# Attention in a two-layer hybrid backbone: queries split once and placed by transfers, the result norm taken for two heads at a time, its epsilon term summed by TensorE

## The chip, the cores and the metric

The kernel runs on one core of a Trainium2 chip. The metric is the time of one execution in device microseconds, as the median of several runs. The engines of the core work side by side, each on its own list of instructions in a fixed order, and wait for each other through semaphores: TensorE (PE in the profile; PEld is its weight load), VectorE (DVE), ScalarE (ACT), GpSimd (POOL) and SyncE (SP), whose list here holds only the starts of transfers.

## The reference, cut to what matters

Two layers of a backbone over 512 latent and 256 context tokens. Between one input projection and one output projection stand three groups of heads; the change touches group B, differential attention with 4 heads of two softmax maps each. In layer 0 the context tokens attend among themselves as well; in the last layer they only give keys and values.

```python
def diff_attn(q, k, v, lam):
    s = jnp.einsum("bqhmd,bkhmd->bhmqk", q.astype(F32), k.astype(F32)) * (B_QK_DIM ** -0.5)
    p = jax.nn.softmax(s, axis=-1)
    a = p[:, :, 0] - lam * p[:, :, 1]
    return jnp.einsum("bhqk,bkhd->bqhd", a, v.astype(F32))

def rms_norm(x, g):
    xf = x.astype(F32)
    y = xf * lax.rsqrt(jnp.mean(xf * xf, axis=-1, keepdims=True) + EPS)
    return (y * g.astype(F32)).astype(x.dtype)

def mixer_merge(pa, o, pc, P, lam_init):
    ...
    yb = (rms_norm(o, P["subln_g"]) * (1.0 - lam_init)).astype(pa.dtype).reshape(b, n, B_WIDTH)
    ...
    return jnp.concatenate([ya, yb, yc], axis=-1) @ P["w_out"]
```

`o` is what attention returns, and `rms_norm(o, subln_g)` is the result norm that the title speaks of.

## The kernel before, in words

A scheduler gives each engine the order of its instructions when the kernel is built, from priorities and a cost model of its own; the order is then fixed. Matrix products with weights or activations in fp32r use a split of each operand into a high part and the rest (`mm3`, L225 to L228: three products), so that every weight tile is loaded as `raw`, cast to `whi` by ACT and has its rest `wlo` taken by DVE or POOL (`wsplit`).

**The attention stage** (L712 to L870) stands once in each layer between the last input projection and the output projection. Its unit of work is a pair (head h, block p of 256 queries), and each pair has two units of 128 queries. Layer 0 has 12 pairs: first the 4 heads of the context block (`p == 2`, 256 keys), then 8 latent pairs (768 keys). Layer 1 has only the 8 latent pairs. The text calls them context pairs and latent pairs.

For each pair:

- `q_prep`: two transposes (L737) put the pair's queries into `pq` in PSUM, with the 64 rows of map 0 above the 64 rows of map 1. `qh` holds the high part of one map twice, in the upper and the lower 64 partitions, and `qlz` holds the rest of one map in the half in which that map's rows stand; the other half of `qlz` is zero (written once, L720 and L724). For this ACT copies `pq` to `qn` (L747), two of the four placing copies run on ACT and two on POOL (L751), and DVE takes two rests (L754, which the trace shows on L106). For the first pair all four copies are ACT's (L741).
- `scores`: for each of the two maps, `pss` = kk·qh (L768) + kk·qlz (L769), the row maximum on DVE (`mx`, L771), the exponential with its sum on ACT (`e`; the trace shows all activations of the helper on L97). `pss` has two buffers.
- `combine`: e0 + cc·e1 on DVE (L787), where `cc` comes from the two sums; POOL fills `dg` (L788), a diagonal with the epsilon of the norm times the squared sum.
- `transp`: transposes of `e` (`pat`, L109), 6 for a latent unit, copied to `ath`: the first four by ACT (L804), the last two by DVE (L806).
- `attn_v`: `po` = vt·ath (L816), copied to `o` and squared to `osq` by ACT (L819, L820), and POOL adds `dg` to it (L821).
- `subln`: `pr` = ones·osq (L828) sums over the 128 features; ACT takes logarithm and exponential, DVE scales (`o`, L831), ACT casts `yBh` (L833), DVE takes the rest `yBl` (L834, on L106 in the trace).

Between these TensorE gets filler: `wout(mp2, (0,), ...)`, the part of the output projection that needs only the other head groups (`yACh`, `yACl`), 12 products of one width for each tile `wo`. Layer 0 has 2 of the 4 column groups as filler, layer 1 has 3. DVE adds each finished `wo` tile to `xT` (L704). After the stage the output projection goes on with its remaining parts.

SP's list holds every transfer in one order. During the stage these are the loads of `w_out` tiles (`raw`, 3 buffers), and behind them, for layer 0, loads of modulation weights (`mraw`).

## Time and profile before

| what | us |
|---|---|
| median of 3 runs | 1638.32 (1637.74 to 1638.40) |
| profiled execution | 1637.72, its span 1635.9 |
| attention stage, layer 0 | 246.5 to 354.7 of the span |
| attention stage, layer 1 | 1143.25 to about 1230 of the span |

The profile is of one execution. A busy share counts the time in which an engine has an instruction under way. TensorE's matmuls overlap, so a duration in its rows is longer than the step from one start to the next; what a matmul costs in a chain is read from the starts. The granted clock is a share of TensorE's full speed.

### The profile page before, as it was taken

The page shows a single profiled execution, that of the slowest core. Times are in us where ns is not written, and L with a number is a line of the kernel's source. Part 1 is how long each engine was busy: PE and PEld are TensorE (multiplying, and loading weights), DVE is VectorE, ACT ScalarE, POOL GpSimd, SP SyncE. Part 2 cuts the span into 40 slices and gives each one's busy share as a digit, 9 for nine tenths or more (in the row PEclk, how much of TensorE's full clock was granted, in tenths as well). Part 3 has the DMA queues.
Part 4 walks back from the last instruction along what each step waited for, and adds up shares of the span by engine and source line. Part 5 has one row for each costly group of instructions (what it writes and reads, how often), then busy time and mean ns, then how long its engine had stood idle before and what let it go on. Part 6 is the DMA issues. An engine that isn't in the chain of part 4 may idle for free.

```text
span 1635.9 us, 20796 instructions
## 1 busy us (share of the span) xinstructions
PE 1574.7 (96%) x8186; PEld 1294.7 (79%) x8186; DVE 1033.9 (63%) x1666; ACT 646.2 (40%) x1098; POOL 178.3 (11%) x158
## 2 busy tenths in 40 slices
PE   7999998999999999999999999779999999999999
PEld 5865776778888888888888878567778788888888
DVE  4597878969999862244333277996987544244433
ACT  5431568753523221133232244255775433123321
POOL 1130224310000000000000023341420000000000
PEclk8999999999999999999999999889999999999999
DMA  8625110014355852111122223221001223332232
GB/s 286 201 96 171 42 62 14 14 64 169 104 193 194 290 192 70 66 65 62 56 65 58 84 87 110 62 65 52 27 27 65 91 90 96 88 101 97 96 100 94
DMA packets 57409, 162.08 MB, mean 99 GB/s; under 512 B 9056, under 2 KB 11360, under 8 KB 57184
## 3 DMA queue, kind: packets, MB, share of 16 engines
q1 hardware_dynamic: 57312, 160.76, 30.3%
q8 instruction: 64, 1.05, 0.3%
q14 instruction: 33, 0.27, 0.0%
HBM read 158.64 MB, written 2.10 MB: 98 GB/s over the span
## 4 chain that ended last, share of the span: by engine, by line
PE 83%; DVE 10%; ACT 4%; issue 1%; DMA 1%; POOL 0%; POOLq 0%; DVEq 0%; SPq 0%; ACTq 0%
PE pp L227 13%; PE pp L226 13%; PE pp L228 13%; PE pd L228 6%; PE pd L226 6%; PE pd L227 6%; PE acc L389 4%; PE acc L390 4%; PE acc L397 3%; DVE cacc L647 3%; PE po L816 2%; PE mr L156 2%; PE wo L226 1%; PE wo L227 1%; PE wo L228 1%
## 5 line engine op out<-in xcount | busy, mean ns | idle before, releaser
L220 ACT CAST whi<-raw 128x1024 fp32r<-128x1024 f32 (+2 forms) x199 | 204.3, 1029 | 550.9 <-PE pp L227 251.0
L106 DVE TENSOR_TENSOR wlo<-raw,whi 128x1024 fp32r<-128x1024 f32 (+1 forms) x163 | 196.9, 1210 | 304.9 <-ACT whi L220 297.4
L227 PE MATMUL pp<-hlo,whi 128*128 128x512 f32 (+1 forms) x1072 | 380.7, 356 | 0.8 <-DVE hlo L266 0.8
L226 PE MATMUL pp<-hhi,whi 128*128 128x512 f32 (+1 forms) x1072 | 379.8, 356 | 1.5 <-ACT whi L220 1.3
L228 PE MATMUL pp<-hhi,wlo 128*128 128x512 f32 (+1 forms) x1072 | 378.9, 354 | 0.0
L226 PEld LDWEIGHTS pp<-hhi,whi 128*128 128x128 f32 x1072 | 201.4, 188 | 35.1 <-ACT whi L220 2.7
L227 PEld LDWEIGHTS pp<-hlo,whi 128*128 128x128 f32 x1072 | 201.5, 188 | 33.0 <-DVE hlo L266 1.5
L228 PEld LDWEIGHTS pp<-hhi,wlo 128*128 128x128 f32 x1072 | 201.5, 188 | 31.0
L106 POOL TENSOR_TENSOR wlo<-raw,whi 128x1024 fp32r<-128x1024 f32 (+1 forms) x36 | 100.3, 2788 | 870.3 <-ACT whi L220 716.9
L228 PE MATMUL pd<-gh,wlo 128*128 128x512 f32 (+1 forms) x550 | 192.4, 350 | 0.6 <-DVE wlo L106 0.6
L226 PE MATMUL pd<-gh,whi 128*128 128x512 f32 (+1 forms) x550 | 192.9, 351 | 0.0
L227 PE MATMUL pd<-gl,whi 128*128 128x512 f32 (+1 forms) x550 | 192.3, 350 | 0.0
L389 PE MATMUL acc<-whi,hhi 128*128 128x512 f32 x352 | 144.8, 411 | 2.8 <-ACT whi L220 2.8
L390 PE MATMUL acc<-whi,hlo 128*128 128x512 f32 x352 | 144.2, 410 | 0.0
L647 DVE SCALAR_TENSOR_TENSOR cacc<-cin,cw,cacc 128x783 f32<-128x783 f32 (+1 forms) x120 | 125.8, 1102 | 2.8 <-ACT cacc L642 2.7
L228 PEld LDWEIGHTS pd<-gh,wlo 128*128 128x128 f32 x550 | 103.4, 188 | 15.9 <-DVE wlo L106 0.8
L227 PEld LDWEIGHTS pd<-gl,whi 128*128 128x128 f32 x550 | 103.5, 188 | 15.1
L226 PEld LDWEIGHTS pd<-gh,whi 128*128 128x128 f32 x550 | 103.4, 188 | 14.9
L983 DVE TENSOR_TENSOR ft<-ft,pp 128x256 f32<-128x256 f32 (+1 forms) x66 | 39.4, 598 | 96.2 <-PE pp L228 84.7
L397 PE MATMUL acc<-wlo,hhi 128*128 128x512 f32 x352 | 94.0, 401 | 0.0
L389 PEld LDWEIGHTS acc<-whi,hhi 128*128 128x128 f32 x352 | 68.0, 193 | 25.0 <-issue 7.1
L192 DVE CUSTOM_DVE_ANT_0 mraw<-mraw,csil,bmod 128x1024 f32<-128x1024 f32 x64 | 81.7, 1280 | 8.0 <-DMA mraw<-in_w_modT_dram 7.8
(198 smaller groups left out, 2334.3 us busy)
## 6 DMA issues: line engine op xcount, KB each, us to landing
raw<-in_w_gv_dram SPq DMA_DIRECT2D x88, 512.0 KB, 3.2
mraw<-in_w_modT_dram SPq DMA_DIRECT2D x64, 512.0 KB, 4.2
raw<-in_w_in_dram SPq DMA_DIRECT2D x44, 512.0 KB, 3.6
raw<-in_w_down_dram SPq DMA_DIRECT2D x34, 512.0 KB, 3.6
mraw<-in_w_modN_dram SPq DMA_DIRECT2D x16, 512.0 KB, 5.9
mraw<-in_w_modH_dram SPq DMA_DIRECT2D x16, 512.0 KB, 3.9
raw<-in_w_out_dram SPq DMA_DIRECT2D x16, 512.0 KB, 3.2
raw<-in_w_down_dram SPq DMA_DIRECT2D x16, 384.0 KB, 3.2
```

What stands on the lines that cost most here:

```text
L106: (eng or V).tensor_sub(o, a, hi.bitcast(F32))
L156: T.matmul(o[r:r + 32], cs[:, k], w, start=k < 4, stop=k >= 4, tile_position=(0, r))
L192: r = V.tensor_tensor_reduce(out=junk, in0=w, in1=csil[:, s], scale=1.0, scalar=bmod[:, l, i, f:f + 1], op0=ALU.mult, op1=ALU.add, accum_o ...
L220: S.copy(hi, raw)
L226: T.matmul(o, lhi, rhi, start=start, stop=False)
L227: T.matmul(o, lhi, rlo, start=False, stop=False)
L228: T.matmul(o, llo, rhi, start=False, stop=stop)
L389: T.matmul(pt[t], hhi[hs], wh[:, a], start=k2 + a == 0, stop=False)
L390: T.matmul(pt[t], hlo[hs], wh[:, a], start=False, stop=False)
L397: T.matmul(pt[t], hhi[hs], wl[:, a], start=False, stop=k2 + 1 == KD // 2 and a == 1)
L647: V.scalar_tensor_tensor(out=cacc[:, c, :cn], in0=cin[:, c, j:j + cn], scalar=cw[:, l, c, j:j + 1], in1=cacc[:, c, :cn], op0=ALU.mult, op1 ...
L983: V.tensor_mul(t[:, a:b], t[:, a:b], pp[s][1][:, :b - a])
```

## The change

The zeroed buffers go. `q_prep` casts the pair's queries once to `qn[:, 0]` (ACT) and takes the rest once to `qn[:, 1]` (DVE); four transfers on the sync queue then place both parts of each map in both halves of `qq`. The rest thus stands in both halves too. `qq` has three buffers and `qn` two. `dg` has 5 buffers instead of 3. In `transp` the second copy (L806 before) goes to ACT for the second unit of each pair. In `attn_v` only the copy to `o` is left, into one half of a tile for two pairs. `subln` runs once for two pairs (two heads of the same block): one square, one logarithm, one exponential, one scaling, one cast and one rest, each 512 wide instead of 256; POOL's addition of `dg` to `osq` goes, and TensorE adds ones·dg into `pr` by a second matmul for each pair.

```diff
-            qlz = [sp.tile([P, 2, 256], F32R, name=f"qlz{x}") for x in range(2)]
-            zero = sp.tile([P, 256], F32, name="zero")
-            G.memset(zero, 0.0)
-            for x in qlz:
-                for m in range(2):
-                    ms = slice((1 - m) * QKD, (2 - m) * QKD)
-                    G.tensor_copy(x[ms, m], zero[ms])
...
             def q_prep(n):
                 h, p = pairs[n]
-                qh = sp.tile([P, 2, 256], F32R, tag="qh", name="qh", bufs=QB)
-                ql = qlz[n % 2]
+                qq = sp.tile([P, 2, 2, 256], F32R, tag="qq", name="qq", bufs=QB)
+                qn = sp.tile([P, 2, 256], F32R, tag="qn", name="qn", bufs=2)
                 pq = ps.tile([P, 256], F32, tag="w", name="pq", bufs=WB)
                 for i in range(2):
                     T.transpose(pq[:, i * P:(i + 1) * P], qt[2 * p + i][:, h * P:(h + 1) * P], ident)
-                if n == 0:
-                    for m in range(2):
-                        for a in range(2):
-                            S.copy(qh[a * QKD:(a + 1) * QKD, m], pq[m * QKD:(m + 1) * QKD])
-                    for m in range(2):
-                        ms = slice(m * QKD, (m + 1) * QKD)
-                        sub_lo(ql[ms, m], pq[ms], qh[ms, m])
-                else:
-                    qn = sp.tile([P, 256], F32R, tag="qn", name="qn", bufs=2)
-                    S.copy(qn, pq)
-                    for m in range(2):
-                        src = qn[m * QKD:(m + 1) * QKD]
-                        for a in range(2):
-                            (G.tensor_copy if a else S.copy)(qh[a * QKD:(a + 1) * QKD, m], src)
-                    for m in range(2):
-                        ms = slice(m * QKD, (m + 1) * QKD)
-                        sub_lo(ql[ms, m], pq[ms], qn[ms])
-                st["q", n] = (qh, ql)
+                S.copy(qn[:, 0], pq)
+                sub_lo(qn[:, 1], pq, qn[:, 0])
+                for m in range(2):
+                    for a in range(2):
+                        nc.sync.dma_start(out=qq[a * QKD:(a + 1) * QKD, :, m].bitcast(F32), in_=qn[m * QKD:(m + 1) * QKD].bitcast(F32))
+                st["q", n] = (qq[:, 0], qq[:, 1])
...
-                    if c0 == 0:
+                    if c0 == 0 or i == 1:
                         S.copy(at[osl], pat[:, :cn_])
                     else:
                         V.tensor_copy(at[osl], pat[:, :cn_])
...
-                o = sp.tile([P, 256], F32, tag="o", name="o", bufs=2)
-                sq = sp.tile([P, 256], F32, tag="osq", name="osq", bufs=2)
-                S.copy(o, po)
+                if n % 2 == 0:
+                    st["sub", n // 2] = sp.tile([P, 2, 256], F32, tag="o", name="o", bufs=2)
+                S.copy(st["sub", n // 2][:, n % 2], po)
+
+            def subln(x):
+                h, p = pairs[2 * x]
+                o = st["sub", x]
+                sq = sp.tile([P, 2, 256], F32, tag="osq", name="osq", bufs=2)
                 S.activation(sq, o, AF.Square)
-                G.tensor_add(sq, sq, st["dg", n].rearrange("p a q -> p (a q)"))
-                st["sub", n] = (o, sq)
-
-            def subln(n):
-                h, p = pairs[n]
-                o, sq = st["sub", n]
-                pr = ps.tile([P, 256], F32, tag="w", name="pr", bufs=WB)
-                T.matmul(pr, ones, sq, start=True, stop=True)
+                pr = ps.tile([P, 2, 256], F32, tag="w", name="pr", bufs=WB)
+                for y in range(2):
+                    T.matmul(pr[:, y], ones, sq[:, y], start=True, stop=False)
+                    T.matmul(pr[:, y], ones, st["dg", 2 * x + y].rearrange("p a q -> p (a q)"), start=False, stop=True)
                 act(sq, pr, AF.Ln, scale=1.0 / P)
                 act(sq, sq, AF.Exp, scale=-0.5)
                 V.scalar_tensor_tensor(out=o, in0=o, scalar=gsub, in1=sq, op0=ALU.mult, op1=ALU.mult)
-                ts = slice(p * 256, p * 256 + 256)
-                S.copy(yBh[:, h, ts], o)
-                sub_lo(yBl[:, h, ts], o, yBh[:, h, ts])
+                osl = (slice(None), slice(h, h + 2), slice(p * 256, p * 256 + 256))
+                S.copy(yBh[osl], o)
+                sub_lo(yBl[osl], o, yBh[osl])
...
-                if 0 <= v < nu and units[v][1] == 1:
-                    subln(units[v][0])
+                if 0 <= v < nu and units[v][1] == 1 and units[v][0] % 2 == 1:
+                    subln(units[v][0] // 2)
```

The order of the other work moves with it, at three places above all. **The start of the stage in layer 0, on TensorE.** A row is line, operation, output and inputs; `pq` are query transposes, `wo` filler, `pss` scores. Before, from the last two transposes on:

```order
L737 MATMUL pq<-ident,q_1271 128x128
L737 MATMUL pq<-ident,q_1272 128x128
L226 MATMUL wo<-yACh,whi 128x256
L227 MATMUL wo<-yACl,whi 128x256
L228 MATMUL wo<-yACh,wlo 128x256
L768 MATMUL pss<-kk,qh 128x256
L226 MATMUL wo<-yACh,whi 128x256
```

Now, at the same place, the end of the filler that stands between the transposes and the first scores:

```order
L228 MATMUL wo<-yACh,wlo 128x512
L226 MATMUL wo<-yACh,whi 128x512
L227 MATMUL wo<-yACl,whi 128x512
L750 MATMUL pss<-kk,qq 128x256
L751 MATMUL pss<-kk,qq 128x256
L228 MATMUL wo<-yACh,wlo 128x512
```

Three filler products stood between the last transpose and the first score; now 20 do, 12 of width 256 and 8 of width 512. In all, 66 filler products of layer 0 (36 of width 256, 30 of width 512) stand ahead of the first latent score now, 18 of width 512 in the latent pairs, and none behind the last score. In layer 1, 16 of width 512 stand ahead of the first score, where 2 did, and 12 behind the last, where 25 did.

**The end of the stage in layer 0, on TensorE.** Here `pat` are transposes of `e`, `po` the products with the values, `pr` the sums of the norm. Before:

```order
L109 MATMUL pat<-ident,e 128x128 x6
L227 MATMUL wo<-yACl,whi 128x512
L228 MATMUL wo<-yACh,wlo 128x512
L816 MATMUL po<-ath,vt 128x256 x6
L828 MATMUL pr<-osq,ones 128x256
L226 MATMUL wo<-yACh,whi 128x512
L227 MATMUL wo<-yACl,whi 128x512
L228 MATMUL wo<-yACh,wlo 128x512
L226 MATMUL wo<-yACh,whi 128x512
L828 MATMUL pr<-osq,ones 128x256
```

Now:

```order
L109 MATMUL pat<-ident,e 128x128 x6
L798 MATMUL po<-ath,vt 128x256 x6
L811 MATMUL pr<-osq,ones 128x256
L812 MATMUL pr<-dg,ones 128x256
L811 MATMUL pr<-osq,ones 128x256
L812 MATMUL pr<-dg,ones 128x256
L226 MATMUL wo<-yACh,whi 128x256
L227 MATMUL wo<-yACl,whi 128x256
```

The filler between and behind the last sums is gone from here, and each pair's sum is followed by the product with `dg`.

**SP's queue in layer 0**, from the last loads of the input projection on. Before:

```order
L212 DMA raw<-in_w_in_dram 128x2x512 x4
L212 DMA raw<-in_w_out_dram 128x1024 x7
L189 DMA mraw<-in_w_modT_dram 128x1024 x2
L212 DMA raw<-in_w_out_dram 128x1024
L189 DMA mraw<-in_w_modT_dram 128x1024
```

Now:

```order
L212 DMA raw<-in_w_in_dram 128x2x512 x4
L212 DMA raw<-in_w_out_dram 128x1024 x5
L736 DMA qq<-qn 64x2x256 x12
L212 DMA raw<-in_w_out_dram 128x1024
L736 DMA qq<-qn 64x2x256 x20
L212 DMA raw<-in_w_out_dram 128x1024
L736 DMA qq<-qn 64x2x256 x16
L189 DMA mraw<-in_w_modT_dram 128x1024 x2
```

The 48 placing transfers of layer 0 stand in one queue with the last two weight loads between them, each of which waits for a `raw` buffer, and ahead of the modulation loads.

## Rows read from the trace of the kernel before

**Rows 1.** The profile page: part 1 (busy time, share of the span and instructions of each engine), and the shares by engine in the chain that ended last.
```profile
PE 1574.7 (96%) x8186; PEld 1294.7 (79%) x8186; DVE 1033.9 (63%) x1666; ACT 646.2 (40%) x1098; POOL 178.3 (11%) x158
...
PE 83%; DVE 10%; ACT 4%; issue 1%; DMA 1%; POOL 0%; POOLq 0%; DVEq 0%; SPq 0%; ACTq 0%
```

**Rows 2.** Busy time by stretch: start and end of the stretch, its length, busy time and instructions of each engine, granted clock, share of the transfer engines, GB/s. First the context pairs, the latent pairs and the tail of layer 0, then start, latent pairs and tail of layer 1.
```profile
246.50:266.90 20.40, 16.32 (x86) 13.04 (x85) 16.36 (x49) 16.78 (x58) 10.87 (x23) 0.83 0.08 27
266.90:339.50 72.60, 67.02 (x370) 55.41 (x370) 67.14 (x128) 57.65 (x140) 24.91 (x38) 1.00 0.03 8
339.50:354.70 15.20, 13.72 (x65) 10.33 (x63) 8.93 (x18) 9.69 (x22) 2.31 (x4) 1.00 0.00 1
...
1143.25:1147.50 4.25, 3.49 (x17) 2.16 (x16) 2.04 (x6) 3.93 (x11) 3.77 (x5) 1.00 0.11 29
1147.50:1219.00 71.50, 67.45 (x364) 55.32 (x363) 66.95 (x123) 54.09 (x124) 25.77 (x39) 1.00 0.06 21
1219.00:1232.80 13.80, 12.90 (x59) 10.25 (x58) 7.58 (x13) 9.19 (x18) 1.45 (x2) 1.00 0.12 39
```

**Rows 3.** The groups of VectorE and ScalarE that the change touches, and one row of a wider kind, in the stage of layer 0 (244 to 354), shapes kept apart: busy time, mean ns of one, then idle time before them.
```profile
L106 DVE TENSOR_TENSOR qlz<-pq,qn 64x256 fp32r<-64x256 f32 x22 | 9.2, 418 | 0.4
L831 DVE SCALAR_TENSOR_TENSOR o<-o,gsub,osq 128x256 f32<-128x256 f32 x12 | 7.1, 594 | 2.9 <-ACT osq L97 2.8
L806 DVE COPY ath<-pat 128x256 f32<-128x256 f32 x16 | 6.5, 413 | 1.7 <-PE pat L109 1.6
L106 DVE TENSOR_TENSOR yBl<-o,yBh 128x256 fp32r<-128x256 f32 x11 | 4.6, 419 | 1.7 <-ACT yBh L833 1.6
L704 DVE SCALAR_TENSOR_TENSOR xT<-wo,modv,xT 128x512 f32<-128x512 f32 x4 | 3.0, 745 | 0.4 <-PE wo L228 0.3
L804 ACT COPY ath<-pat 128x256 f32<-128x256 f32 x8 | 3.0, 371 | 1.3 <-PE pat L109 1.2
L751 ACT CAST qh<-qn 64x256 fp32r<-64x256 f32 x22 | 8.9, 404 | 0.3
L747 ACT CAST qn<-pq 128x256 fp32r<-128x256 f32 x11 | 4.0, 378 | 0.6 <-PE pq L737 0.5
```

**Rows 4.** A subtraction of width 512 on VectorE, from its timeline: start, duration, engine, line.
```profile
374.30 0.69 DVE L249 TENSOR_TENSOR nss<-nss,nsq 128x512 f32<-128x512 f32 x1
```

**Rows 5.** POOL's addition to the squares in the same stretch of layer 0, in the form of rows 3, and from the list of waits TensorE's for POOL's placing copies (us in total, times, longest).
```profile
L821 POOL TENSOR_TENSOR osq<-osq,dg 128x256 f32<-128x256 f32 x12 | 10.6, 885 | 23.8 <-ACT osq L820 23.8
...
PE pss L768 <- POOL qh L751: 1.6, 2, 1.1
```

**Rows 6.** TensorE's timeline in the tail of layer 0: start, duration, line, operation, and in brackets what ended an idle time ahead of it. `x12`, `x2` count the instructions of a row; an fp32 product of the program is two of them.
```profile
342.17 2.86 PE L816 MATMUL po<-ath,vt 128*128 128x256 f32 x12
344.86 0.59 PE L828 MATMUL pr<-osq,ones 128*128 128x256 f32 x2
345.30 0.82 PE L109 MATMUL pat<-ident,e 128*128 128x128 f32 x6
345.87 0.48 PE L227 MATMUL wo<-yACl,whi 128*128 128x512 f32 x1
...
351.32 0.70 PE L828 MATMUL pr<-osq,ones 128*128 128x256 f32 x2 [0.41 <-POOL osq L821]
...
352.31 0.40 PE L226 MATMUL wo<-yACh,whi 128*128 128x512 f32 x1
352.55 0.40 PE L227 MATMUL wo<-yACl,whi 128*128 128x512 f32 x1
...
354.71 0.39 PE L226 MATMUL wo<-yACh,whi 128*128 128x256 f32 x1 [0.84 <-DVE xT L704]
```

**Rows 7.** TensorE's timeline over one latent pair of layer 0, from one pair's first score after a sum to the next: its two ends, its filler and its idle time.
```profile
298.66 0.58 PE L768 MATMUL pss<-kk,qh 128*128 128x512 f32 x1
...
301.06 0.48 PE L228 MATMUL wo<-yACh,wlo 128*128 128x512 f32 x1
...
301.83 0.48 PE L226 MATMUL wo<-yACh,whi 128*128 128x512 f32 x1
...
302.38 0.40 PE L228 MATMUL wo<-yACh,wlo 128*128 128x512 f32 x1
303.77 0.47 PE L768 MATMUL pss<-kk,qh 128*128 128x512 f32 x1 [0.99 <-ACT e L97]
...
308.50 0.58 PE L768 MATMUL pss<-kk,qh 128*128 128x512 f32 x1
```

**Rows 8.** TensorE's timeline ahead of the stage in layer 0, two filler products of width 256, and the first complete scores of layer 1.
```profile
245.08 0.28 PE L226 MATMUL wo<-yACh,whi 128*128 128x256 f32 x1
245.20 0.28 PE L227 MATMUL wo<-yACl,whi 128*128 128x256 f32 x1
...
1143.25 0.82 PE L737 MATMUL pq<-ident,q 128*128 128x128 f32 x6
...
1146.69 0.51 PE L769 MATMUL pss<-kk,qlz 128*128 128x512 f32 x1 [0.72 <-POOL qlz L724]
```

**Rows 9.** Transfers: tensors, queue, count, KB each, median us from issue to landing; and from SP's timeline two issues in a row (start, duration).
```profile
out_dram<-xT SPq DMA_DIRECT2D x4, 128.0 KB, 1.8
lq<-in_lam_qk_dram SPq DMA_DIRECT2D x2, 128.0 KB, 3.7
...
357.13 0.90 SPq L189 DMA_DIRECT2D mraw<-in_w_modT_dram  x2
```

More of the change, by code (lines that the diff above doesn't have):

```diff
@@ L781, in combine @@
                 if i == 0:
-                    st["dg", n] = sp.tile([P, 2, P], F32, tag="dg", name="dg", bufs=3)
+                    st["dg", n] = sp.tile([P, 2, P], F32, tag="dg", name="dg", bufs=5)
                 dg = st["dg", n][:, i]
```

## The prediction

> **What bounds the kernel now.** I read the page first: TensorE is busy for 96% of the span and makes 83% of the chain that ended last [rows 1]. The change touches only the two attention stages, so next I read those by stretch [rows 2]. There TensorE shares the load with VectorE. In the latent pairs of layer 0 TensorE is busy for 67.02 of 72.6 us and VectorE for 67.14, in layer 1 for 67.45 and 66.95 of 71.5; in the context pairs TensorE is busy for 16.32 of 20.4 us and runs at a granted clock of 0.83. From 246.5 to 354.7 TensorE is idle for 4.08 + 5.58 + 1.48 = 11.1 us, in layer 1 for 0.76 + 4.05 + 0.90 = 5.7 us. The pair in [rows 7] shows the kind of idle time: 0.99 us until ACT has read a score buffer, which it can only do after VectorE's maximum. So there are 16.8 us to win at most, plus what the lower clock costs; all else in the two stages is TensorE's own work.
>
> **VectorE's part.** For a latent pair the change takes away one copy of 413 ns, replaces two rests of 418 ns by one of 128x256 (nearest row: `yBl`, 419 ns), and halves the count of `o` and `yBl` while doubling their width. The wide scaling is bounded by the 745 ns of a 512-wide one that reads PSUM, the wide rest by 0.69 us [rows 3, 4]. Per two pairs these go from 2 x 594 + 2 x 419 = 2026 to 745 + 690 = 1435 ns, or -0.30 us a pair. Together: 0.41 + 0.42 + 0.30 = 1.13 us a latent pair, 0.72 a context pair, 16 x 1.13 + 4 x 0.72 = 21 us. VectorE falls to about 58 of 72.6 us in layer 0's latent pairs and is then no longer the second bound. None of this is on the path by itself: it pays only as far as TensorE's idle time shrinks.
>
> **ScalarE and POOL.** Per latent pair ScalarE loses two placing copies of 404 ns and gains one copy of 371 ns [rows 3]; logarithm, square, exponential and cast are merged. It was busy for 57.65 of 72.6 us [rows 2] and gets less, so I cost it at nothing; its cover is VectorE's and TensorE's load, and without that one more copy ahead of an exponential would cost 0.4 us a pair. POOL's 885 ns additions go, and with them TensorE's waits for POOL, 0.41 us ahead of the last sum [rows 6] and 1.6 us for placing copies [rows 5].
>
> **TensorE's part.** The epsilon term adds one fp32 product of width 256 for each pair. Its row exists: `pr` starts at 344.86 and the next work at 345.30, so 0.44 us [rows 6]. That is 12 x 0.44 = 5.3 us in layer 0 and 8 x 0.44 = 3.5 in layer 1, 8.8 us on the engine that bounds. This is the price of the change, and it is certain.
>
> **TensorE's need, counted by starts.** A latent pair takes 308.50 - 298.66 = 9.84 us, of which four filler products (0.93, at 0.233 each by [rows 6]) and 1.1 us of idle time, so 7.8 us net [rows 7]. A context pair needs 8 score products of width 256 at 0.12 [rows 8], 4 transposes at 0.095, two products of `po` at 0.45, a sum and two query transposes: 0.96 + 0.38 + 0.90 + 0.44 + 0.19 = 2.9 us (transposes from 345.30 to 345.87, `po` from 342.17 to 344.86 for six [rows 6]). Filler in layer 0 behind the first transposes: 36 x 0.12 + 48 x 0.233 = 15.5 us.
>
> - Layer 0 now: 4 x 2.9 + 8 x 7.8 + 15.5 + 5.3 = 94.8 us of the 108.2 that it takes today. What stays idle I estimate from the order. At the start 12 x 0.12 + 8 x 0.233 = 3.3 us of filler stand between the transposes and the first score, and the score needs `qn` (0.38), the rest (0.42), two issues at 0.45 and a landing. The nearest rows for a transfer of 128 KB say 1.8 us (from SBUF) and 3.7 us [rows 9]; I take 1.8, since these too read SBUF and little else is moving (27 GB/s in [rows 2]). That gives 0.38 + 0.42 + 0.45 + 1.8 = 3.1 us behind the transpose, and 0.9 more for the second map: some 1 us of waiting. I add 1.5 for the rest of the context pairs, 0.3 a latent pair (2.4; today 0.7 by [rows 2]), and 2 in the tail, where the last sums now wait for a copy and a 512-wide square with no filler beside them. 94.8 + 6.9 = 101.7, or -6.5 us.
> - Layer 1, to the fixed point at 1232.8: 8 x 7.8 + 84 x 0.233 + 3.5 = 85.5 us. Ahead of the first scores stand 16 x 0.233 = 3.7 us of filler, which reach the same 1147 at which today's first complete score comes, late for POOL's zeroing (0.72) [rows 8]. With 3.2 us idle it is 88.7 against 89.55: -0.9 us.
>
> **The other end, counted by busy time.** Busy time holds small waits that starts don't show as idle. By [rows 2], layer 0's context pairs need 12.8 us at full clock (16.32 less half of the 6.9 us at half speed), and take 8.5 us more filler (36 x 0.12 + 30 x 0.233 = 11.3, where 2.8 stood): about +2.5 with the waits. The latent pairs lose 3.8 us of filler and gain 3.5 of sums, so only 5.58 us of idle time can go, of which I leave 1.4: -4.2. The tail loses 20 filler products (4.7) and gains 4 products and a sum (2.2) and 0.5 of waiting: -2.0. Layer 1: +3.5 and 2.9 of its 5.7 us idle won: +0.6. Sum: -3.1 us.
>
> Between -7.4 and -3.1 I take -4.5, nearer the second, because it comes from rows over whole stretches and the first rests on one pair. The profiled execution took 1637.72 us (1635.9 of span and 1.8 around it), 0.6 below the median; on the median of 1638.32 the forecast is **1633.8 us**.
>
> **A rule weighed.** By [rows 9] I cost the landing of a placing transfer at 1.8 us. The Trainium skill ("DMA: Bandwidth & Descriptors", section on the anatomy of one DMA) gives, for another way of issuing, a fixed part of about 2.0 us plus bytes over 436e3; as an estimate by that page this is 2.3 us for 128 KB, and would add 0.5 us at the start of each stage, 1 us in all. No transfer inside SBUF is in this trace, so neither is shown.
>
> **The rivals.**
>
> - *TensorE pays and gets nothing back* (slower). VectorE's share falls, but the idle time was never its load: it is the round from scores over maximum and exponential back to one of two `pss` buffers, which the change leaves as it was, and the filler that used to stand in the latent pairs is used up early. Against it: VectorE was busy for 92% of those stretches, which leaves its queue no slack for that round. Price with the idle times of today: layer 0 +2.5 and 1.0 at the start, latent pairs -0.3, tail -2.0, layer 1 +3.5, so +4.7: 1643 us. It decides when more than about 12 of the 16.8 us idle remain.
> - *The transfers come late.* At 3.7 us to landing a first score comes 5 us behind its transpose and the second map's 6, so the 3.3 and 3.7 us of filler don't cover it: 2 to 2.5 us at each start. Context pairs 3 and 4 have some 5.5 to 6.5 us of TensorE's work between transposes and first score, where queueing on ScalarE and VectorE (an exponential and a maximum) adds up to 2 us to the 6: 1 to 2 us more. Latent pairs have 7.5 us or more and are covered. A transfer also stands behind weight loads that wait for a `raw` buffer, but in the order the casts that free these stand ahead of the query copies whose transfers come behind the load. Sum +5 on the forecast: 1638.5 us, no change. For it: two of the rows for this size say 3.2 us or more; against it: those ran among other loads.
> - *More than forecast.* TensorE runs its list without idle time in the latent pairs, and the clock stays up in the context pairs since filler now stands there: -9 us, 1629 us.
> - *The relief is beside the point*, both ends cancel within 3 us. That lies inside the first two, no case of its own.
>
> **How the numbers follow.** Forecast 0.50, TensorE pays 0.16, late transfers 0.20, more than forecast 0.14. What a measurement of this kernel can tell from no change is about 0.2%, 3.3 us: 1635.0 is the line. A fifth of the forecast's own spread (1630 to 1637) lies above it: faster 0.40 + 0.14 = 0.54. Same: 0.10 + 0.17 of the late transfers + 0.03 of the slower rival = 0.30; slower 0.16. The range leaves out the outer half of the slower rival and the best of the last one: 1628 to 1642.
>
> **What would show each step.** Right: VectorE busy near 58 us in the latent stretch of layer 0, `pr` twice as many products at 0.44 us each, TensorE idle there below 3 us, stage of layer 0 at 103 to 106 us and layer 1's within 1 us of today's. Wrong: TensorE waiting for `qq` from a transfer by more than 2 us in all; idle time for ACT's `e` as large as now; a granted clock below 0.9 in a context or tail stretch, which would cost up to 3.5 us there.

## Result, and the profile after

The changed kernel takes 1646.31 us (median of 4 runs, 1645.87 to 1647.4) against 1638.24 for the kernel before on the same chip: a ratio of 1.0051, 95% interval 1.0033 to 1.0068. It is 8 us slower; 1633.8 was forecast. The profiled execution has a span of 1644.3 us, 8.4 more than before.

The page of the changed kernel, part 1 and the chain's shares by engine, which answer to [rows 1]: all engines but TensorE have less to do, TensorE has 7.4 us more, and its share of the chain rises from 83 to 85%.

```profile
PE 1582.1 (96%) x8226; PEld 1302.5 (79%) x8226; DVE 1015.5 (62%) x1610; ACT 631.7 (38%) x1032; POOL 140.0 (9%) x92
...
PE 85%; DVE 9%; ACT 3%; issue 1%; DMA 1%; POOL 1%; SPq 0%; DVEq 0%; ACTq 0%
```

To find where the time went I cut each stage in three, at marks that every kernel here has: **start**, from the first query transposes to the first score; **middle**, from there to the last score; **tail**, from there to the first 512-wide filler product behind the products with `yBh`. Busy time by stretch for the kernel before, columns as in [rows 2]; first layer 0 (start, middle, tail), then layer 1:

```profile
246.51:247.72 1.21, 1.21 (x11) 0.99 (x9) 0.48 (x1) 0.76 (x3) 1.21 (x1) 1.00 0.00 0
247.72:339.23 91.51, 81.84 (x445) 67.18 (x443) 82.74 (x174) 73.51 (x195) 34.29 (x60) 0.96 0.04 12
339.23:360.63 21.40, 19.91 (x116) 16.41 (x115) 11.25 (x21) 11.31 (x26) 2.58 (x4) 1.00 0.13 48
1143.25:1144.46 1.21, 1.21 (x9) 0.84 (x8) 0.75 (x2) 1.07 (x4) 0.91 (x1) 1.00 0.00 0
1144.46:1213.64 69.18, 65.21 (x349) 53.03 (x349) 63.03 (x117) 53.11 (x124) 27.11 (x42) 1.00 0.05 16
1213.64:1235.61 21.97, 20.23 (x95) 16.11 (x94) 13.77 (x22) 13.03 (x26) 2.98 (x3) 1.00 0.25 76
```

The same six stretches of the changed kernel:

```profile
246.12:252.17 6.05, 4.53 (x28) 3.53 (x27) 1.72 (x4) 0.65 (x2) 1.26 (x1) 1.00 0.57 172
252.17:342.35 90.18, 83.30 (x459) 68.67 (x460) 75.94 (x149) 65.54 (x158) 13.10 (x23) 1.00 0.32 77
342.35:362.57 20.22, 17.10 (x106) 14.96 (x105) 7.49 (x12) 11.46 (x21) 0.45 (x1) 1.00 0.15 53
1144.40:1152.05 7.65, 4.81 (x23) 3.41 (x22) 2.17 (x5) 0.97 (x3) 2.40 (x1) 0.93 0.48 147
1152.05:1221.94 69.89, 67.42 (x351) 55.82 (x352) 56.81 (x95) 47.31 (x102) 12.41 (x16) 0.96 0.27 67
1221.94:1243.57 21.63, 20.02 (x95) 15.61 (x93) 10.98 (x17) 12.82 (x22) 1.25 (x1) 1.00 0.22 74
```

Layer 0: +4.84, -1.33, -1.18, together +2.33 us. Layer 1: +6.44, +0.71, -0.34, together +6.81. What lies before, between and behind the stages adds -0.4, -0.8 and +0.4. So the starts cost 11.3 us, and middles and tails are only 2.1 us shorter. They lost filler worth 3.3 and 3.7 us to the starts, but took in 20 epsilon products, 8.6 us by their rows, and a half clock in layer 1 (below) for the one that the kernel before had in layer 0 (0.96). VectorE's relief came (82.74 to 75.94 us in layer 0's middle); these sums don't show what it bought.

TensorE's timeline at the first score of layer 0 and at the start of layer 1, changed kernel (start, duration, and in brackets what ended an idle time):

```profile
252.17 0.36 PE L750 MATMUL pss<-kk,qq 128*128 128x256 f32 x1 [0.94 <-DMA qq<-qn]
...
1147.61 0.39 PE L228 MATMUL wo<-yACh,wlo 128*128 128x512 f32 x1
1148.84 0.50 PE L226 MATMUL wo<-yACh,whi 128*128 128x512 f32 x1 [0.84 <-DVE xT L704]
...
1152.05 0.76 PE L750 MATMUL pss<-kk,qq 128*128 128x512 f32 x1 [2.00 <-DMA qq<-qn]
1152.61 0.63 PE L751 MATMUL pss<-kk,qq 128*128 128x512 f32 x1
...
1157.31 0.60 PE L227 MATMUL wo<-yACl,whi 128*128 128x512 f32 x1
1157.73 0.41 PE L750 MATMUL pss<-kk,qq 128*128 128x512 f32 x1
```

After 0.84 and 2.00 us of idle time the products take 0.63 us where they took 0.39: from 1152.05 to 1157.31 the granted clock is 0.50, the lower of its two levels (1.2 GHz), which costs half of that stretch, 2.6 us. SP's timeline at the same place:

```profile
1138.73 8.73 SPq L212 DMA_DIRECT2D raw<-in_w_out_dram  x2
1147.52 10.05 SPq L736 DMA_DIRECT2D qq<-qn  x12
```

The placing transfers of the whole program (an issue's shortest, median and longest time in ns, then the first and last start):

```profile
L736 SPq DMA_DIRECT2D qq<-qn x80: 590/607/1432, 247.8 to 1209.3; - x80
...
DMA to landing us min/median/max: 2.3/2.4/4.5
```

The same for the first four of layer 0 (247 to 250), then of layer 1 (1147.4 to 1150):

```profile
L736 SPq DMA_DIRECT2D qq<-qn x4: 610/644/814, 247.8 to 249.8; - x4
DMA to landing us min/median/max: 3.4/3.5/3.6
```

```profile
L736 SPq DMA_DIRECT2D qq<-qn x4: 599/608/632, 1147.5 to 1149.5; - x4
DMA to landing us min/median/max: 3.5/3.7/3.9
```

And the transfers from 1140 to 1165, with the median us to landing last:

```profile
qq<-qn SPq DMA_DIRECT2D x12, 128.0 KB, 3.2
raw<-in_w_out_dram SPq DMA_DIRECT2D x2, 512.0 KB, 3.4
```

In layer 1 the queries are cast and their rest taken by 1145.65, but SP stands at a weight load until 1147.13. Then it issues the load and behind it the placing transfers at 0.6 us each, and their data share the engines with that load. The longest issue, 1.43 us, stands in the middle of layer 1 and not here.

### The profile page after: what moved, and what is told of

Read it like the earlier page. It is cut to its first block, busy times and chain, and to the rows that moved or that the text cites. A ratio compares the mean times of both kernels' runs of the same rounds, so it can differ in the third digit from the quotient of the medians.

```text
span 1644.3 us, 20831 instructions
## 1 busy us (share of the span) xinstructions
PE 1582.1 (96%) x8226; PEld 1302.5 (79%) x8226; DVE 1015.5 (62%) x1610; ACT 631.7 (38%) x1032; POOL 140.0 (9%) x92
## 4 chain that ended last, share of the span: by engine, by line
PE 85%; DVE 9%; ACT 3%; issue 1%; DMA 1%; POOL 1%; SPq 0%; DVEq 0%; ACTq 0%
PE pp L227 13%; PE pp L226 13%; PE pp L228 13%; PE pd L228 6%; PE pd L227 6%; PE pd L226 6%; PE acc L389 3%; DVE cacc L647 3%; PE acc L390 3%; PE acc L397 3%; PE po L798 3%; PE wo L226 2%; PE wo L227 2%; PE wo L228 2%; PE mr L156 2%; PE pss L750 1%
```

## The experiments

Times are medians; the ratio is to the kernel before on the same chip, with its 95% interval. The parts are read from starts in the one profile of each kernel, as above, in us. In e1 the mark that ends layer 1's tail comes five `yBh`/`yBl` products early, so that about 1.2 us are missing from that tail.

| kernel | us | ratio | layer 0: start, middle, tail | layer 1: start, middle, tail |
|---|---|---|---|---|
| before | 1638.24 | 1 | 1.21, 91.51, 21.40 | 1.21, 69.18, 21.97 |
| changed | 1646.31 | 1.0051 (1.0033 to 1.0068) | 6.05, 90.18, 20.22 | 7.65, 69.89, 21.63 |
| e1, epsilon on POOL | 1639.70 | 1.0013 (1.0004 to 1.0022) | 6.17, 87.76, 21.12 | 7.81, 65.30, 19.37 |
| e2, placed by engines | 1640.59 | 1.0023 (1.0013 to 1.0033) | 1.21, 92.96, 22.79 | 1.22, 70.07, 22.19 |
| e3, before + TensorE epsilon | 1649.09 | 1.0067 (1.0054 to 1.0080) | 1.21, 91.80, 29.36 | 1.22, 68.96, 27.01 |
| e4, before + transfers | 1638.67 | 1.0008 (0.9999 to 1.0017) | 6.00, 88.06, 18.49 | 7.63, 66.43, 18.66 |
| e5, wide norm and copy alone | 1637.26 | 0.9996 (0.9987 to 1.0005) | 1.21, 90.11, 22.62 | 1.21, 68.46, 22.06 |
| e6, narrow norm | 1645.03 | 1.0046 (1.0033 to 1.0058) | 6.05, 91.43, 18.65 | 7.64, 70.53, 18.80 |
| e7, epsilon in fp32r | 1639.67 | 1.0009 (1.0000 to 1.0018) | 6.17, 89.31, 18.96 | 7.74, 68.73, 19.59 |
| e8, first pair by engines | 1633.43 | 0.9971 (0.9961 to 0.9982) | 1.21, 90.72, 19.36 | 1.22, 67.45, 23.61 |
| e9, e8 + e7 | 1630.17 | 0.9949 (0.9937 to 0.9962) | 1.22, 89.78, 17.63 | 1.21, 66.17, 22.35 |
| e10, e8 + e1 | 1630.74 | 0.9952 (0.9940 to 0.9965) | 1.21, 90.86, 20.55 | 1.21, 65.56, 22.68 |
| e11, first pair on ACT's queue | 1648.31 | 1.0059 (1.0046 to 1.0071) | 7.40, 91.51, 20.22 | 4.77, 71.45, 21.74 |
| e12, changed kernel again | 1647.01 | 1.0056 (1.0040 to 1.0071) | 6.23, 90.41, 20.22 | 7.62, 68.88, 21.62 |

I began with two theories: P, TensorE pays for the epsilon products, and T, the transfers are late.

**e1.** Epsilon back on POOL.

```diff
+                for y in range(2):
+                    G.tensor_add(sq[:, y], sq[:, y], st["dg", 2 * x + y].rearrange("p a q -> p (a q)"))
...
-                    T.matmul(pr[:, y], ones, sq[:, y], start=True, stop=False)
-                    T.matmul(pr[:, y], ones, st["dg", 2 * x + y].rearrange("p a q -> p (a q)"), start=False, stop=True)
+                    T.matmul(pr[:, y], ones, sq[:, y], start=True, stop=True)
```

> The changed kernel with POOL adding dg to the squares again, so that TensorE's 20 epsilon products go and all else stays. Theory P (TensorE pays): its trace shows 0.43 us from one product with dg to the next start, 20 x 0.43 = 8.6 us on the engine that bounds, so 1646.3 - 8.6 = 1637.7 us. Theory T (the transfers do it): the idle time that TensorE has in the two stages takes most of these products, the sums in the tail wait for POOL's 0.9 us addition instead, and the loss stays: 1643 to 1646 us.

1639.70, 6 to 7 us below the changed kernel, nearer P. But the starts are as late as ever, and most of the gain in layer 1's middle (4.59 us, where the products of four pairs are 1.7) is the clock: here it stayed at 1.00 behind the same idle time, so that the row which answers to 1152.05 above is short:

```profile
1150.04 0.47 PE L750 MATMUL pss<-kk,qq 128*128 128x512 f32 x1 [2.16 <-DMA qq<-qn]
```

**e2.** The `q_prep` of before, with its zeroed buffers, in the changed kernel.

```diff
-                S.copy(qn[:, 0], pq)
-                sub_lo(qn[:, 1], pq, qn[:, 0])
...
-                        nc.sync.dma_start(out=qq[a * QKD:(a + 1) * QKD, :, m].bitcast(F32), in_=qn[m * QKD:(m + 1) * QKD].bitcast(F32))
+                            (G.tensor_copy if a else S.copy)(qh[a * QKD:(a + 1) * QKD, m], src)
...
+                        sub_lo(ql[ms, m], pq[ms], qn[ms])
```

> The changed kernel with the queries placed by ScalarE and POOL and the rests taken twice, as before the change; epsilon on TensorE, wide result norm and ScalarE's copy stay. Theory P: the placing is not what costs, 1645 to 1648 us. Theory T: the waits at the start go (0.94 us in layer 0; 0.84 + 2.00 in layer 1 and some 2.5 us at a granted clock of 0.50 behind them) and filler comes back to the tails, where sums and transposes now wait 3.1 us in layer 0; some of that is given back to VectorE's two rests, so 1638 to 1641 us.

1640.59, some 5 us below, for T. Each edit alone takes back over half of the loss of 0.0051: 0.0038 and 0.0028. Added up that is 0.0066; e5 below has both edits and takes back 0.0055, which is the same within the intervals. So whether the two hang together is not shown here.

**e3.** Only the epsilon term in the kernel before.

```diff
-                G.tensor_add(sq, sq, st["dg", n].rearrange("p a q -> p (a q)"))
...
-                T.matmul(pr, ones, sq, start=True, stop=True)
+                T.matmul(pr, ones, sq, start=True, stop=False)
+                T.matmul(pr, ones, st["dg", n].rearrange("p a q -> p (a q)"), start=False, stop=True)
```

> The kernel before with nothing changed but the epsilon term: POOL's addition goes, TensorE sums ones x dg into pr for each head (dg with 5 buffers). Theory P: 1638.2 + 8.6 - 1 for the waits on POOL = 1646 us. Theory T: at most a third of the loss, 1639 to 1641 us.

1649.09, more than P asked for, and not where P put it. The middles are unchanged (+0.29, -0.22), though the products of nine and five pairs lie there, 3.9 and 2.2 us by their rows; but 16 filler products (2.4 us) left layer 0's middle and two (0.5 us) layer 1's, while layer 0's middle has 3.4 us more at half clock than before (0.94 for 0.96). The tails are 8.0 and 5.0 us longer. They hold the other products (three each), the filler that left the middles, 3.4 us each at half clock (0.94), and more idle time (4.5 and 2.8 us for 1.5 and 1.7): filler stands bunched behind the last sums and waits for VectorE's additions. TensorE's waits in layer 0's tail (us in total, times, longest):

```profile
PE wo L226 <- DVE xT L704: 4.2, 2, 2.9
```

So this run prices an order of the filler and the clock beside the products, not the products alone.

**e4.** Only the transfers in the kernel before.

```diff
-                            (G.tensor_copy if a else S.copy)(qh[a * QKD:(a + 1) * QKD, m], src)
...
+                S.copy(qn[:, 0], pq)
+                sub_lo(qn[:, 1], pq, qn[:, 0])
...
+                        nc.sync.dma_start(out=qq[a * QKD:(a + 1) * QKD, :, m].bitcast(F32), in_=qn[m * QKD:(m + 1) * QKD].bitcast(F32))
```

> The kernel before with nothing changed but the queries: one cast, one rest and four transfers on the sync queue. Theory P: VectorE's relief and the waits cancel, 1637 to 1640 us. Theory T: both starts are late as in the changed kernel and the filler is used up early, 1643 to 1646 us.

1638.67: within P's range, but not for P's reason. The starts are late by 4.79 and 6.42 us, as T said, and in the profiled execution (1635.84 us, where the runs go from 1634.90 to 1642.34) all of it comes back: middles -3.45 (the half clock of before's context pairs is gone, 3.4 us) and -2.75, tails -2.91 and -3.31, about the filler that had been done in the starts. In the changed kernel that return is missing. The question was now what takes it.

**e5.** The changed kernel with e1's and e2's edits, so that only the wide norm and ScalarE's copy are left of the change. Against the kernel before:

```diff
-                    if c0 == 0:
+                    if c0 == 0 or i == 1:
                         S.copy(at[osl], pat[:, :cn_])
...
+                S.copy(st["sub", n // 2][:, n % 2], po)
...
+                pr = ps.tile([P, 2, 256], F32, tag="w", name="pr", bufs=WB)
```

> The kernel before with only the wide result norm and ScalarE's copy: engines place the queries, POOL adds epsilon. VectorE is relieved of 0.30 + 0.41 us a latent pair, 11 us in all, at no price on TensorE. Theory R (relief of VectorE pays, as the prediction had it): 2 to 4 us below the kernel before. Theory N (TensorE's idle time in the pairs is not VectorE's load; the trace of the changed kernel has 75.1 - 69.2 = 5.9 us of it in layer 0's latent pairs with VectorE at 84%, where the kernel before has 5.6 with VectorE at 92%): within 1 us of the kernel before, or up to 2 above for the wide sums of the last two heads.

1637.26, no difference. Theory N: the page has VectorE busy for 1026.2 us where 1033.9 stood, 7.7 us less and not 11, and that is worth 0.8 us in the stages. The middles are 1.40 and 0.72 us shorter, the tails 1.22 and 0.09 longer. The page, part 1:

```profile
PE 1573.7 (96%) x8186; PEld 1292.6 (79%) x8186; DVE 1026.2 (63%) x1630; ACT 646.6 (40%) x1074; POOL 178.1 (11%) x158
```

**e6.** The norm for each head, as before, with an epsilon product for each.

```diff
-                if n % 2 == 0:
-                    st["sub", n // 2] = sp.tile([P, 2, 256], F32, tag="o", name="o", bufs=2)
-                S.copy(st["sub", n // 2][:, n % 2], po)
+                o = sp.tile([P, 256], F32, tag="o", name="o", bufs=2)
+                sq = sp.tile([P, 256], F32, tag="osq", name="osq", bufs=2)
+                S.copy(o, po)
+                S.activation(sq, o, AF.Square)
```

> The changed kernel with the result norm for each head by itself; transfers, TensorE's epsilon and ScalarE's copy stay. If the wide norm is what makes the tails late (the last sums wait 1.12 us for a 512-wide square in each layer and the products behind 0.9 us for the last wide rest in layer 1): 3 to 4 us below the changed kernel, 1642 us. If it is only the missing filler and the epsilon: within 1.5 us of it, and VectorE and ScalarE get 0.3 us a pair more to do.

1645.03, 1 us below. The tails are 1.57 and 2.83 us shorter, the middles 1.25 and 0.64 longer. The wide norm does lengthen a tail that has no filler, by about what was expected of the tails, and gives 1.89 of the 4.40 us back in the middle. That leaves 2.5 us in the stages; the time shows 1, since the profiled execution was 1.3 us longer ahead of and between the stages, where the two kernels are the same.

**e7.** Epsilon products as one instruction.

```diff
+            onesr = sp.tile([P, P], F32R, name="onesr")
+            G.tensor_copy(onesr, ones)
...
-                    st["dg", n] = sp.tile([P, 2, P], F32, tag="dg", name="dg", bufs=5)
+                    st["dg", n] = sp.tile([P, 2, P], F32R, tag="dg", name="dg", bufs=5)
...
-                    T.matmul(pr[:, y], ones, st["dg", 2 * x + y].rearrange("p a q -> p (a q)"), start=False, stop=True)
+                    T.matmul(pr[:, y], onesr, st["dg", 2 * x + y].rearrange("p a q -> p (a q)"), start=False, stop=True)
```

> The changed kernel with dg and its ones in fp32r, so that each epsilon product should take one instruction like the 256-wide filler at 0.12 us instead of 0.43; the order of TensorE's filler is the same as in the changed kernel. If the epsilon's price is its own duration: 20 x 0.31 = 6.2 us less, 1640 us. If the idle time takes it and the loss is the late starts: within 2 us of the changed kernel.

1639.67, the 6.2 us and no less (0.0042 by the ratios, 6.9 us; 5.1 in the stages of the profiles). The last two sums of layer 0 on TensorE's timeline, first the changed kernel, then e7:

```profile
355.03 0.70 PE L811 MATMUL pr<-osq,ones 128*128 128x256 f32 x2 [1.12 <-ACT osq L808]
355.56 0.59 PE L812 MATMUL pr<-dg,ones 128*128 128x256 f32 x2
356.00 0.59 PE L811 MATMUL pr<-osq,ones 128*128 128x256 f32 x2
```

```profile
354.80 0.70 PE L813 MATMUL pr<-osq,ones 128*128 128x256 f32 x2 [1.12 <-ACT osq L810]
355.15 0.47 PE L814 MATMUL pr<-dg,onesr 128*128 128x256 f32 x1
355.45 0.60 PE L813 MATMUL pr<-osq,ones 128*128 128x256 f32 x2
```

From sum to sum it is 0.97 us there and 0.65 here. Starts, middles and tails hold the same number of filler products as in the changed kernel, and the half clock of layer 1 is as long, so this is close to the price of the products there. The order is not quite the same, though the expectation took it to be: in layer 0's latent pairs the last dozen filler products stand one to two pairs later.

**e8.** The first pair of each stage by engines, from PSUM; the rest by transfers.

```diff
+                if n == 0:
+                    for m in range(2):
+                        ms = slice(m * QKD, (m + 1) * QKD)
+                        for a in range(2):
+                            S.copy(qq[a * QKD:(a + 1) * QKD, 0, m], pq[ms])
+                        for a in range(2):
+                            sub_lo(qq[a * QKD:(a + 1) * QKD, 1, m], pq[ms], qq[ms, 0, m])
+                    st["q", n] = (qq[:, 0], qq[:, 1])
+                    return
```

> The changed kernel with the first pair of each stage placed by four copies of ScalarE and four rests of VectorE from PSUM; all other pairs by transfers. If the transfers' first landing is what costs (6.05 and 7.65 us from transposes to the first score, against 1.21): the waits of 0.9 and 2.8 us and the 2.6 us at half clock go, 5 to 6 us less, 1640 us. If the second pair's transfers then stand late in the same way, or the lateness is made up by filler later: within 2 us of the changed kernel.

1633.43: 13 us below the changed kernel and 4.6 below the kernel before, twice what was expected. Its six stretches, in the form above:

```profile
246.66:247.87 1.21, 1.21 (x12) 0.99 (x10) 0.51 (x2) 0.76 (x3) 1.21 (x1) 1.00 0.00 0
247.87:338.59 90.72, 85.62 (x479) 70.94 (x477) 76.65 (x153) 65.91 (x161) 13.09 (x24) 1.00 0.33 82
338.59:357.95 19.36, 16.84 (x107) 14.93 (x106) 8.40 (x14) 11.57 (x21) 0.51 (x1) 1.00 0.15 55
1140.15:1141.37 1.22, 1.22 (x10) 0.85 (x8) 0.78 (x3) 1.07 (x4) 0.92 (x1) 1.00 0.00 0
1141.37:1208.82 67.45, 65.44 (x353) 53.76 (x353) 59.86 (x102) 48.22 (x105) 14.44 (x17) 1.00 0.31 79
1208.82:1232.43 23.61, 22.35 (x108) 18.05 (x106) 11.74 (x16) 13.05 (x22) 0.45 (x1) 1.00 0.14 48
```

The starts are short again, and the filler that had stood in them now stands behind the first score. Middle and tail of layer 0 hold 85.62 + 16.84 = 102.46 us of TensorE's work against 100.40 in the changed kernel, and take 110.08 us against 110.40. There the moved filler runs where TensorE had waited; done ahead of the first score it had saved nothing. Layer 1 is different: 12 of the 14 products moved went to the tail, which is 1.98 us longer, and the middle is 2.44 us shorter, about what the half clock had cost (2.6 us). So the filler done early had saved some 2 us there.

**e9 and e10.** e8 with e7's edit, and e8 with e1's: the line of TensorE that differs from e8, first e9's, then e10's.

```diff
-                    T.matmul(pr[:, y], ones, st["dg", 2 * x + y].rearrange("p a q -> p (a q)"), start=False, stop=True)
+                    T.matmul(pr[:, y], onesr, st["dg", 2 * x + y].rearrange("p a q -> p (a q)"), start=False, stop=True)
...
+                    G.tensor_add(sq[:, y], sq[:, y], st["dg", 2 * x + y].rearrange("p a q -> p (a q)"))
```

> The first pair of each stage placed by engines and the epsilon products in fp32r (dg and its ones), otherwise the changed kernel. Its two edits each took away part of the loss by themselves. The trace shows 0.31 us less for each epsilon product (0.86 against 0.55 us from one product with osq to the next), 20 x 0.31 = 6.2 us. Theory: where TensorE's filler no longer stands ahead of late scores the engine is the bound and pays each product in full, so 1633.4 - 6.2 = 1627 us. Rival: in the latent pairs TensorE waits for exponentials anyway, and those products cost only where nothing waits: 1631 us.

> The first pair placed by engines and epsilon added on POOL; the rest as in the changed kernel, with filler in nearly the same places. Theory (TensorE pays each product): 1633.4 - 8.6 = 1625 us, plus up to 1 for the sums that wait for POOL's additions in the tails. Rival (idle time takes them): 1630 to 1633 us.

1630.17 and 1630.74. In fp32r the stages shrink by 2.66 and 2.55 us of 6.2 that left TensorE, the ratio by 0.0022, 3.6 us: between theory and rival. (The profile of e9 has a half clock that e8's lacks, 3.4 us long at the end of layer 0's latent pairs; without it the stages would have shrunk by 1.7 us more.) On POOL layer 1 gains 2.83 us, layer 0 loses 1.33: its granted clock is 0.96 and 0.92 in middle and tail, and a sum waits 2.0 us for POOL. e9 and e10 are the fastest here, 8.4 and 7.8 us below the kernel before; the 0.6 us between them is within the noise.

**e11.** The first pair's transfers from ScalarE's queue.

```diff
-                        nc.sync.dma_start(out=qq[a * QKD:(a + 1) * QKD, :, m].bitcast(F32), in_=qn[m * QKD:(m + 1) * QKD].bitcast(F32))
+                        (nc.scalar if n == 0 else nc.sync).dma_start(out=qq[a * QKD:(a + 1) * QKD, :, m].bitcast(F32), in_=qn[m * QKD:(m + 1) * QKD].bitcast(F32))
```

> The changed kernel with the first pair's four transfers of each stage issued from ScalarE's queue, which is idle there, instead of the sync queue; everything else on the sync queue. If the first score is late because these transfers stand behind a weight load (1.9 us in layer 1, 0.4 in layer 0) and behind each other's issue, it comes 1 to 2 us earlier in layer 1, the idle time there falls from 2.8 us to about 1, and the time by 2 to 5 us with the clock: 1642 us. If it is issue and landing themselves, little changes: 1645 to 1646 us.

1648.31, no gain. In layer 1 the first score comes 2.88 us earlier, but the second map's then waits for its own transfers, in a stretch in which the transfer engines are 0.96 busy. TensorE's timeline, and below it busy time by stretch, 0.96 being the share of the transfer engines:

```profile
1152.40 0.39 PE L750 MATMUL pss<-kk,qq 128*128 128x512 f32 x1
...
1156.38 0.47 PE L750 MATMUL pss<-kk,qq 128*128 128x512 f32 x1 [2.21 <-DMA qq<-qn]
```

```profile
1150.00:1155.00 5.00, 3.34 (x15) 2.13 (x13) 1.71 (x2) 0.00 (x0) 0.34 (x1) 1.00 0.96 234
```

In layer 0 the start got longer (7.40). The Trainium skill ("DMA: Bandwidth & Descriptors", section on rules for kernel authors) says that spreading transfers over issuing engines doesn't help bandwidth and only saves issue time. This run agrees: issues went from one queue to two, and the time stayed (1648.31 against 1646.31, intervals that overlap).

**e12.** The changed kernel once more, without an edit.

> The changed kernel once more, for a second profile: if the half clock behind the idle time at layer 1's start belongs to this order of work, it is there again, at the same place and for about 5 us; if it came by chance, not. Time 1646 us.

1647.01. The late starts are the same to 0.2 us. The half clock is there again but shorter, by the clock in two stretches of 5 us:

```profile
1150.00:1155.00 5.00, 3.03 (x10) 2.17 (x9) 1.01 (x2) 0.39 (x2) 0.00 (x0) 0.76 0.91 234
1155.00:1160.00 5.00, 3.87 (x17) 2.97 (x16) 3.19 (x6) 3.62 (x7) 1.97 (x2) 0.90 0.48 108
```

That is a loss of (0.24 + 0.10) x 5 = 1.7 us. The same two stretches have 0.59 and 0.73 in the first profile of the changed kernel (3.4 us, part of it in idle time) and 0.69 and 0.62 in e6 (3.4). In e1 and e4 there was no fall at layer 1's start. The lateness belongs to the order; the clock's fall comes and goes, and is 0 to 3.4 us of the loss.

## Why the prediction was wrong, point by point

- **The step that failed: the starts.** The prediction gave them "some 1 us of waiting" in layer 0 and none in layer 1, because 3.3 and 3.7 us of filler stand between transposes and first score. That priced a late first score by TensorE's idle time alone and took filler for cover. The starts cost 4.84 and 6.44 us. In the changed kernel and e8 layer 0 takes 90.18 and 90.72 us from first to last score, with 83.3 and 85.6 us of work on TensorE: the last score is late by nearly all that the first one is late by, and filler spent ahead of it was no gain. That the round from scores to exponentials sets this pace is argued from such figures, not shown; the length is no constant (87.8 in e1, 88.1 in e4). e8, which takes away the late first score and what follows from it, is worth 5.16 + 6.89 = 12.05 us in the stages, of which 2.6 are the half clock, and 13 us in the time: more than the whole loss.
- **The same, by pairs of kernels.** Six kernels with the wide norm and ScalarE's copy differ in two things only, who places the queries and who adds epsilon. Their ratios:

| epsilon | all pairs by engines | all by transfers | first pair by engines, rest by transfers |
|---|---|---|---|
| on POOL | 0.9996 (e5) | 1.0013 (e1) | 0.9952 (e10) |
| on TensorE | 1.0023 (e2) | 1.0051 (changed) | 0.9971 (e8) |

Placing the first pair by transfers too costs 0.0061 and 0.0080 (10 and 13 us). With an early first pair the transfers gain 0.0044 and 0.0052 over engines (7 and 8.5 us), so the queries' part of the change does pay, until the late start eats it. Epsilon on TensorE costs 0.0019 to 0.0038 (3 to 6 us), where 8.8 was forecast. Each difference is uncertain by 2 to 3 us. Without epsilon's 8.8 us the forecast stood 13.3 us below the kernel before; e10 is 7.9 below it and e1, with the late first pair, 2.1 above. So the late start is 10 of the 15 us missed there; the rest is relief that was sized too large.
- **The size of the lateness.** 3.1 us behind the transposes were forecast; it is 5.3 in layer 0 (252.17 less 246.86, the first filler behind them) and 7.1 in layer 1 (1152.05 less 1144.98). An issue takes 0.6 us, not 0.45. A landing takes 2.4 us in the median of all 80, but 3.5 and 3.7 for the first four of each stage, beside a weight load, not 1.8. And in layer 1 SP stood 1.5 us longer at a load that waited for a `raw` buffer, which the prediction had held to be free in time. The 2.3 us that the prediction worked out from the Trainium skill ("DMA: Bandwidth & Descriptors", section on the anatomy of one DMA, for another way of issuing) as an estimate is near the median, but not near the landings that count here; by itself it would have changed the forecast by 1 us.
- **The rival "transfers come late"** had the mechanism, the wait at both starts, the 3.7 us to landing, and 5 us for it (its sum should read 1638.8, not 1638.5). It too counted waits.
- **VectorE's relief.** It came nearly as costed: 18.4 us less on the page, for 21. In the latent stretch of the changed kernel VectorE was busy for 63.31 of 75.10 us, 84% where 80 was forecast and 92 had been:

```profile
266.90:342.00 75.10, 69.23 (x376) 57.25 (x375) 63.31 (x113) 55.54 (x125) 9.96 (x17) 1.00 0.28 65
```

But TensorE's idle time there is 5.87 us, not below 3, and its waits for `e` in layer 0 are 5.4 us against 6.2. e5 shows the norm's and the copy's part to be worth under 1 us; the queries' part pays with an early first pair, as the table says, but it also takes load off ScalarE and POOL, and no run separates these. For the changed kernel the slower rival was right that most of that idle time stays; that it is the round's is not shown.
- **The epsilon term.** 0.44 us a product was forecast, 0.43 is its row. "Certain" was too strong: removing 0.31 us of each gave all 6.2 us in the changed kernel (e7), but 3.6 in the time and 5.2 in the stages with early scores (e9).
- **The tails.** Filler gone, the wide square's wait is 1.12 us in each layer, and in layer 1 the products wait again for the last wide cast and rest (0.29 and 0.50 us at 1241.56 and 1242.29). The forecast of -2.0 for layer 0 became -1.18. With a narrow norm (e4, e6) an early spent filler does shorten the tail, by 3 us each. That, the epsilon products and the half clock stand between e4, where what the transfers gain and what the late starts cost cancel, and the changed kernel.
- **The context pairs' clock.** Granted 1.00 in layer 0 from start to end of the stage, as the last rival hoped, where 0.83 stood in [rows 2]. The clock fell in layer 1 instead.
- **That e8 takes 1633.4 us** and 1633.8 was forecast doesn't make the other terms right: in the stages its gain over before is 2.83 us in layer 0 and 0.08 in layer 1, where the count by busy time had -3.7 and +0.6, and the half clock that before had in layer 0 (3.4 us) is gone. It is the sum of a smaller gain than forecast and a cheaper epsilon term: luck.

Open: what decides whether the clock falls behind the same idle time in layer 1. And in e8 and e10 the filler's order moves with the first pair; the late score was not delayed alone with the order held, so what the order itself is worth is not known.

## What to carry to other kernels

Where a stage is a round between engines, ask when its first step can start. Here 11 us of lateness at the two starts cost 10 to 13 us, and independent work done meanwhile was worth only what it would have cost later: nothing in layer 0, some 2 us in layer 1. Prepare the first item of such a stage by the shortest path, even a wasteful one, and give the cheap but slow path (a transfer) to the items behind it. Relieving an engine that is 90% busy promises nothing by itself: 7.7 us less on VectorE were worth 0.8 us in e5. Look for a wait that ends on it first.

## What the runs showed of the hardware

- A placing transfer inside SBUF (64 partitions, two rows of 1 KB each, 128 KB) took 0.59 to 1.43 us to issue on the sync queue, median 0.61, where a 512 KB weight load took 0.33, and landed in 2.3 to 4.5 us, median 2.4; the first four of each stage, issued right behind a weight load, took 3.4 to 3.9.
- At the start of layer 1 the granted clock fell to 0.50 within or behind idle times of 0.84 and 1.97 to 2.21 us in the changed kernel, e6, e7, e11 and e12, and stayed at 1.00 behind 0.84 and 2.04 to 2.16 us in e1 and e4.
- Of the 6.2 us that 20 products gave up on an engine which was 96% busy, between half (3.6 in e9) and all (e7) showed in the time.
